# Linear attention's rows multiplied by their gates in an earlier stage of a hybrid encoder layer

## The chip, the cores and the metric

The kernel runs on one core of a Trainium2 chip. A core has five engines with an instruction stream each: TensorE (PE; its weight loads are listed apart as PEld), VectorE (DVE), ScalarE (ACT), GpSimd (POOL) and SyncE (SP). SP issues nearly all of the transfers (DMAs) of this kernel. An engine runs its instructions in order and waits where one of them needs what is not there yet. The metric is the device time of one execution in microseconds (us); less is better.

## The reference, cut to what matters

One inference step of an encoder layer with two groups of heads side by side: latent attention and gated linear attention. 1024 tokens of a new stream and 64 of a running one go through it together, 1088 in all. The width is 1024; each group gives 512 of the 1024 columns that the output projection reads.

```python
def gla_mixer(q, k, v, gate_lr, r, s0, ...):
    ...
    o, s_new = gla_recurrence(q, k, v, log_a, s0)
    o = rms_norm(o, g_gla_out.reshape(GLA_HEADS, GLA_DV))
    return o.reshape(B, T, GLA_WIDTH) * silu(r), s_new

def encoder_layer(x, c, ...):
    ...
    proj = h @ w_in                       # q latents, key latents, rotary key, GLA's q, k, v, gates, r
    a_out, latent_new, krope_new = mla_mixer(...)
    b_out, s_new = gla_mixer(gq, gk, gv, g_lr, g_r, ...)
    x = x + gate1 * (concatenate([a_out, b_out]) @ w_out)
    h2 = rms_norm(x, g_norm2) * (1 + scale2) + shift2
    x = x + gate2 * (square(relu(h2 @ w_up)) @ w_down)
```

The change is about `* silu(r)`: 512 rows by 1088 tokens, multiplied elementwise before `w_out`.

## The kernel before

Activations are kept transposed: features on the 128 partitions, tokens along the free axis. A float32 product is made of three matmuls of rounded parts (`mm3`, L94 to L96): `split` (L102, L103) rounds the operand on ACT to a high part and subtracts it on DVE for a low part.

Stages follow each other: the input projection, linear attention with the key latents, the query latents' stage (262 to 345 us), attention (345 to 540), the output projection with the second norm (540 to some 640), the MLP up and down (to the end). Within a stage, generators ("streams") yield a TensorE price, a time to wait and a condition; `interleave` (L47) takes the first that is ready by its own count and so writes out the order of the work. The scheduler below it moves instructions on an engine unless they are pinned by `keep_in_program_order`. The order is fixed when the kernel is built, and so is the order in which SP issues transfers.

Two tensors in DRAM carry the columns for the output projection. `mix_d` holds 8 blocks of 128 rows: blocks 0 to 3 are attention's results, not yet divided by the sums of their rows, whose reciprocals lie in `rs_d`; blocks 4 to 7 are linear attention's normalized results, without `silu(r)`. `r_d` holds `r`.

- **`gates()`** (L1371), a stream of the latents' stage: four steps of 272 tokens. A step loads `r` (four blocks, two places), takes Silu on ACT (L1379) and stores it back to `r_d` (L1380). Behind the last step ACT loads the table for exponentials. Beside it on the engines: `cn` and `lat` (the normalized key latent, L701, L705), `cl`, which goes to `lat_d` and comes back as `latr` for the keys; `kn`, `kl`, `kh`, `kr` (keys, L996 to L1025), `cq` (query latents, L1365), stored to `cq_d`. TensorE transposes `cn` (L715) and the keys (L1014).
- **`out_early()`** (L1284), a stream of the attention stage: the first 272 tokens of the output projection's operand are loaded, multiplied by their factor (`gate`, L1278: attention's rows by `rs_d`, the others by `r_d`), and split.
- **`main()`** (L1442): the output projection in four turns `w` of 272 tokens (`WORDER`, 0, 2, 1, 3). A turn has `mx` (two tiles of four blocks; four places, so two turns), `mr` (the gates, two places) and `mb` (the reciprocals for attention's rows, one place). `gate(mx[0], mb)` and `gate(mx[1], mr)` run on DVE as products of 128x1088, then `split` makes `mh` and `ml`. While turn `w` runs, the loads of `mr`, `mb` and `x` for turn `w + 1` and of `mx` for `w + 2` are issued.
- **`norm2()`**: per turn, the sum of squares `acc` becomes `st` (DVE L1526, a power on POOL L1527), `dg` (DVE L1530: a diagonal), and a matmul of `dg` (L1534) that spreads it over the partitions.

Of the kernel before, what the change touches and what calls it, by code (L numbers as in the profile page):

```python
# [10 lines left out]
F32 = mybir.dt.float32  # L11
# [3 lines left out]
ALU = mybir.AluOpType  # L15
# [4 lines left out]
P = 128  # L20
# [6 lines left out]
H = 4  # L27
# [45 lines left out]
def layer(ctx: ExitStack, tc: tile.TileContext, I, O):  # L73
# [1209 lines left out]
    def out_early():  # L1283
# [18 lines left out]
        r1, t3 = fetch(r_d, 0, 2), fetch(mix_d, 3, 1)  # L1302
        yield 0, 2500, None
        pin(gate(t1, r1))
        halves(4, 2, t1)
        t2, r2 = fetch(mix_d, 6, 2), fetch(r_d, 2, 2)
# [3 lines left out]
        pin(gate(t2, r2))  # L1310
# [60 lines left out]
    def gates():  # L1371

        yield 0, 0, has("k 8", "end C1")
        for c in range(4):
            r = qp.tile([P, 4, HT // 2], F32, name="r", bufs=2)
            ts = slice(c * HT // 2, (c + 1) * HT // 2)
            SP.dma_start(r, r_d[:, :, ts])
            yield 0, 3500, None
            ACT.activation(r, r, AF.Silu)  # L1379
            SP.dma_start(r_d[:, :, ts], r)  # L1380
            yield 0, 1000, None
        tc.keep_in_program_order(ACT.preload_act_table_set("natural_log_exp_and_others"))
# [43 lines left out]
    with ExitStack() as octx:  # L1426
# [13 lines left out]
        def main():  # L1440
            ld = {}
# [10 lines left out]
            def load_gates(w):  # L1452
                if w >= 4:
                    return
                c = WORDER[w]
                ld[c] += [xw.tile([P, 4, HW], F32, name="mr", bufs=2), xw.tile([P, 4, HW], F32, name="mb", bufs=1)]
                for _, t0, n, o in place(c)[2]:
                    SP.dma_start(ld[c][3][:, :, o:o + n], sums_row(0, H, t0, n))
                    SP.dma_start(ld[c][2][:, :, o:o + n], r_d[:, :, t0:t0 + n])
# [11 lines left out]
            for w, c in enumerate(WORDER):  # L1471
                _, _, parts = place(c)
                if w == 0:
                    mh, ml = mixh[1]
                else:
                    mx = ld.pop(c)
                    mh, ml = mix_pair() if w == 2 else [xw.tile([P, 8, HW], F32R, name=f"m{x}1", bufs=1) for x in "hl"]
                    gate(mx[0], mx[3])
                    split(mh[:, 0:4], ml[:, 0:4], mx[0], DVE)
                    gate(mx[1], mx[2])  # L1480
                    split(mh[:, 4:8], ml[:, 4:8], mx[1], DVE)
                if w == 0:
                    load_x(0)
                    load_mix(1)
                load_gates(w + 1)
                load_x(w + 1)
                load_mix(w + 2)
# [588 lines left out]
```

## Time and profile before

| | us |
|---|---|
| median of 3 runs | 1329.35 |
| lowest and highest | 1327.03, 1332.3 |
| the profiled execution | 1331.06 |
| its span | 1329.2 |
| PE busy in it | 1307.7 (98%) |
| DVE busy | 911.7 (69%) |
| ACT busy | 647.2 (49%) |
| latents' stage, 262 to 345 us: PE busy, DMA share | 81.25 of 83, 0.53 |
| out projection, 538 to 600 us: PE busy, DMA share | 59.28 of 62, 0.94 |

The span runs from the first to the last instruction of the profiled execution; its time has some 1.9 us more around it. Each row of the engines' timelines begins with the start and the duration in us; a bracket at its end tells how long the engine was idle before the instruction and which instruction or transfer ended that. A row of transfers gives their count, the KB of each and, where the trace tells it, the median us from issue to landing.

### The profile page before, as it was taken

Reading aid. Unit: us, or ns where it says so; the run is one execution under the profiler, and the core shown is the slowest. Engines: PE = TensorE matmul, PEld = TensorE weight load, DVE = VectorE, ACT = ScalarE, POOL = GpSimd, SP = SyncE. Lnnn points to the kernel's source line nnn. Section 1 sums busy time; section 2 is a strip of 40 time slices with the busy share of each in tenths; the row PEclk is TensorE's granted clock in tenths of the full one; section 3 lists DMA queues with packets and bytes.
Section 4 is the critical chain, followed back from the end, with each engine's and each line's share of the span. In section 5 each row is a group of like instructions: output and inputs, shape, how many; then the busy total and the mean of one; then the engine's idle time right before and its main releaser. Section 6 shows DMA issues by size and latency. Waiting matters only on the chain.

```text
span 1329.2 us, 25834 instructions
## 1 busy us (share of the span) xinstructions
PE 1307.7 (98%) x9925; PEld 1248.1 (94%) x9925; DVE 911.7 (69%) x2032; ACT 647.2 (49%) x1608; POOL 77.7 (6%) x136
## 2 busy tenths in 40 slices
PE   9999999999999999999999999999999999999999
PEld 8899999889777889999999999999999999999998
DVE  4898787466577767576999976566546955864554
ACT  5375554564266666443765445444444343333332
POOL 0100010121112200001000000000000000000000
PEclk9999999999999999999999999999999999999999
DMA  9420123384445202792346654344259645442441
GB/s 344 147 75 1 49 77 89 97 238 128 158 131 155 74 16 81 203 283 86 99 150 210 196 172 157 124 158 140 86 206 384 223 160 193 161 127 85 135 127 35
DMA packets 164653, 191.40 MB, mean 144 GB/s; under 512 B 15686, under 2 KB 116914, under 8 KB 164402
## 3 DMA queue, kind: packets, MB, share of 16 engines
q1 hardware_dynamic: 162002, 186.46, 44.3%
q10 hardware_dynamic: 2528, 3.29, 0.7%
q8 instruction: 78, 1.28, 0.4%
q14 instruction: 45, 0.37, 0.1%
HBM read 136.22 MB, written 53.49 MB: 143 GB/s over the span
## 4 chain that ended last, share of the span: by engine, by line
PE 73%; DVE 11%; DMA 7%; ACT 5%; issue 2%; POOL 2%; SPq 0%; ACTq 0%; DVEq 0%; POOLq 0%
PE mm L94 13%; PE mm L96 12%; PE mm L95 12%; PE g L94 5%; PE g L96 5%; PE g L95 5%; PE tp L94 3%; PE tp L96 3%; PE tp L95 3%; PE mm L1094 3%; PE g L1124 2%; PE g L886 1%; PE mm L179 1%; DMA mb<-rs_d 1%; PE tp L1134 1%
## 5 line engine op out<-in xcount | busy, mean ns | idle before, releaser
L102 ACT CAST opers<-quad 128x512 fp32r<-128x512 f32 x112 | 69.5, 621 | 183.3 <-PE mm L96 147.0
L103 DVE TENSOR_TENSOR opers<-quad,opers 128x512 fp32r<-128x512 f32 x112 | 77.3, 690 | 113.7 <-ACT opers L102 113.7
L96 PE MATMUL mm<-opers 128*128 128x272 f32 x448 | 128.7, 288 | 0.0
L94 PE MATMUL mm<-opers 128*128 128x272 f32 x448 | 128.4, 287 | 0.3 <-DVE e L2003 0.3
L95 PE MATMUL mm<-opers 128*128 128x272 f32 x448 | 128.2, 286 | 0.0
L94 PE MATMUL mm<-ah,wh 128*128 128x272 f32 x424 | 121.8, 288 | 0.0
L96 PE MATMUL mm<-ah,wl 128*128 128x272 f32 x424 | 121.8, 288 | 0.0
L95 PE MATMUL mm<-al,wh 128*128 128x272 f32 x424 | 121.7, 287 | 0.0
L94 PE MATMUL mm<-hh,wh 128*128 128x384 f32 (+2 forms) x264 | 90.7, 344 | 0.1
L95 PE MATMUL mm<-hl,wh 128*128 128x384 f32 (+2 forms) x264 | 87.4, 331 | 0.0
L96 PE MATMUL mm<-hh,wl 128*128 128x384 f32 (+2 forms) x264 | 87.0, 330 | 0.0
L94 PEld LDWEIGHTS mm<-opers 128*128 128x128 f32 x448 | 84.5, 189 | 0.5 <-issue 0.5
L96 PEld LDWEIGHTS mm<-opers 128*128 128x128 f32 x448 | 84.2, 188 | 0.0
L95 PEld LDWEIGHTS mm<-opers 128*128 128x128 f32 x448 | 84.1, 188 | 0.0
L94 PEld LDWEIGHTS mm<-ah,wh 128*128 128x128 f32 x424 | 79.9, 188 | 0.0
L95 PEld LDWEIGHTS mm<-al,wh 128*128 128x128 f32 x424 | 79.7, 188 | 0.0
L103 DVE TENSOR_TENSOR opers<-ru,opers 128x544 fp32r<-128x544 f32 x108 | 77.7, 720 | 2.9 <-ACT opers L102 2.7
L96 PEld LDWEIGHTS mm<-ah,wl 128*128 128x128 f32 x424 | 79.6, 188 | 0.1
L102 ACT CAST opers<-ru 128x544 fp32r<-128x544 f32 x108 | 69.6, 645 | 14.0 <-PE mm L96 10.9
L102 ACT CAST wh<-ru 128x512 fp32r<-128x512 f32 x67 | 41.2, 620 | 66.4 <-PE tp L95 21.0
L94 PE MATMUL mm<-wh,hh 128*128 128x264 f32 (+3 forms) x216 | 65.7, 304 | 0.9 <-ACT cl L718 0.9
L96 PE MATMUL g<-opers 128*128 128x272 f32 x224 | 64.7, 289 | 0.0
(415 smaller groups left out, 4228.5 us busy)
## 6 DMA issues: line engine op xcount, KB each, us to landing
ru<-u_d SPq DMA_DIRECT2D x108, 272.0 KB, 2.8
raw<-in_w_ada SPq DMA_DIRECT2D x32, 512.0 KB, 5.3
ru<-in_w_up SPq DMA_DIRECT2D x32, 512.0 KB, 4.2
quad<-in_w_down SPq DMA_DIRECT2D x16, 1024.0 KB, 5.4
u_d<-st SPq DMA_DIRECT2D x60, 272.0 KB, 2.1
u_d<-sc SPq DMA_DIRECT2D x45, 272.0 KB, 2.2
raw<-in_w_in SPq DMA_DIRECT2D x22, 256.0 KB, 6.1
x<-in_xo_T SPq DMA_DIRECT2D x8, 544.0 KB, 7.9
```

Of the source, the lines that this page charges most:

```text
L94: pin(PE.matmul(out, lhsT=ah, rhs=bh, start=first, stop=False, skip_group_check=more))
L95: pin(PE.matmul(out, lhsT=ah, rhs=bl, start=False, stop=False, skip_group_check=more))
L96: pin(PE.matmul(out, lhsT=al, rhs=bh, start=False, stop=last, skip_group_check=more))
L102: ACT.copy(hi, src)
L103: eng.tensor_tensor(out=lo, in0=src, in1=f32(hi), op=ALU.subtract)
L179: mm = PE.matmul(acc[32 * j:32 * j + 32, 0:256], lhsT=scT[:, k, :], rhs=was[k][:, 256 * j:256 * (j + 1)], start=(k == 0), stop=(k == KT - ...
L886: PE.matmul(sc[:n, a, p], lhsT=d[:, w * p + n * a:w * p + n * a + n], rhs=qv[:, :, p, a], start=True, stop=True)
L1094: PE.matmul(sp[:n, :w], lhsT=x[:, hd, :n], rhs=y[:, hd, :w], start=(j == 0), stop=(j == 4))
L1124: PE.matmul(op[:, :n], lhsT=kvs[kt // 4].v[:kw, kt % 4, hd], rhs=pt[:kw, k, :n], start=(kt == 0), stop=(kt == nkt - 1))
L1134: PE.transpose(tp[:kw, k, :n], pr[k0 // 4][:n, P * k:P * k + kw], ident[:n, :n])
```

## The change

- `gates()` takes eight steps of 136 tokens instead of four of 272. A step loads `r` (two places, as before) and `rm`, linear attention's rows out of `mix_d` (one place), takes Silu of `r` on ACT, multiplies `rm` by it on DVE (L1381) and stores the product back to `mix_d` (L1382). Nothing is stored to `r_d` any more.
- `out_early()` loads no gates, and its two products with them are gone.
- `main()` loads no `mr`; the three products with it are gone. `mb` has three places instead of one. It is loaded two turns ahead, before the `mx` of that turn: the second turn's at the start, ahead of `load_mix(1)`.

```diff
     def gates():
 
         yield 0, 0, has("k 8", "end C1")
-        for c in range(4):
-            r = qp.tile([P, 4, HT // 2], F32, name="r", bufs=2)
-            ts = slice(c * HT // 2, (c + 1) * HT // 2)
+        for c in range(8):
+            r = qp.tile([P, 4, HT // 4], F32, name="r", bufs=2)
+            ts = slice(c * HT // 4, (c + 1) * HT // 4)
+            m = qp.tile([P, 4, HT // 4], F32, name="rm", bufs=1)
             SP.dma_start(r, r_d[:, :, ts])
-            yield 0, 3500, None
+            SP.dma_start(m, mix_d[:, 4:8, ts])
+            yield 0, 2500, None
             ACT.activation(r, r, AF.Silu)
-            SP.dma_start(r_d[:, :, ts], r)
+            yield 0, 1000, None
+            DVE.tensor_tensor(out=m, in0=m, in1=r, op=ALU.mult)
+            SP.dma_start(mix_d[:, 4:8, ts], m)
             yield 0, 1000, None
...
         b0, t0, t1 = fetch(rs_d, 0, 3), fetch(mix_d, 0, 3), fetch(mix_d, 4, 2)
         fetch(rs_d, 3, 1, b3)
         yield 0, 5000, None
         pin(gate(t0, b0))
         halves(0, 3, t0)
-        r1, t3 = fetch(r_d, 0, 2), fetch(mix_d, 3, 1)
+        t3 = fetch(mix_d, 3, 1)
         yield 0, 2500, None
-        pin(gate(t1, r1))
         halves(4, 2, t1)
-        t2, r2 = fetch(mix_d, 6, 2), fetch(r_d, 2, 2)
+        t2 = fetch(mix_d, 6, 2)
         pin(gate(t3, b3))
         halves(3, 1, t3)
         yield 0, 3000, None
-        pin(gate(t2, r2))
         halves(6, 2, t2)
...
-            def load_gates(w):
+            def load_sums(w):
                 if w >= 4:
                     return
                 c = WORDER[w]
-                ld[c] += [xw.tile([P, 4, HW], F32, name="mr", bufs=2), xw.tile([P, 4, HW], F32, name="mb", bufs=1)]
+                rows[c] = xw.tile([P, 4, HW], F32, name="mb", bufs=3)
                 for _, t0, n, o in place(c)[2]:
-                    SP.dma_start(ld[c][3][:, :, o:o + n], sums_row(0, H, t0, n))
-                    SP.dma_start(ld[c][2][:, :, o:o + n], r_d[:, :, t0:t0 + n])
+                    SP.dma_start(rows[c][:, :, o:o + n], sums_row(0, H, t0, n))
...
-                    gate(mx[0], mx[3])
+                    gate(mx[0], rows.pop(c))
                     split(mh[:, 0:4], ml[:, 0:4], mx[0], DVE)
-                    gate(mx[1], mx[2])
                     split(mh[:, 4:8], ml[:, 4:8], mx[1], DVE)
                 if w == 0:
                     load_x(0)
+                    load_sums(1)
                     load_mix(1)
-                load_gates(w + 1)
                 load_x(w + 1)
+                load_sums(w + 2)
                 load_mix(w + 2)
```

SP in the latents' stage, where the third and the fourth step of the gates run (`kraw` is the rotary key, `latr` the key latents coming back). Before, with the loads and the stores of both steps in pairs:

```order
L1377 DMA r<-r_d 128x4x272 x2
L709 DMA out_kr_p<-kraw 128x64
L719 DMA lat_d<-cl 256x1x128
L955 DMA latr<-lat_d 128x2x128
L1380 DMA r_d<-r 512x1x272 x2
L719 DMA lat_d<-cl 256x1x128
L709 DMA out_kr_p<-kraw 128x64
```

Now, from the third step's load of `rm` to the fourth step's store (`r` is loaded a step ahead):

```order
L1376 DMA r<-r_d 128x4x136
L1377 DMA rm<-mix_d 128x4x136
L1382 DMA mix_d<-rm 128x4x136
L719 DMA lat_d<-cl 256x1x128
L709 DMA out_kr_p<-kraw 128x64
L1376 DMA r<-r_d 128x4x136
L1377 DMA rm<-mix_d 128x4x136
L955 DMA latr<-lat_d 128x2x128
L1382 DMA mix_d<-rm 128x4x136
```

Each store of `rm` now stands ahead of the next load of `rm`, and the transfers of the keys stand between them in the same queue.

DVE in the same stage, between the keys (`kn`, `krt`) and two key latents (`cn`, `lat`). Before:

```order
L1007 TENSOR_TENSOR kn<-kn,ssk 128x256
L1008 TENSOR_TENSOR krt<-kraw,ssk 128x256
L701 TENSOR_SCALAR cn<-mm,s_3438 128x256
L705 TENSOR_TENSOR lat<-cn,gkv_bc 128x256
L1365 TENSOR_SCALAR cq<-mm,vT 128x320
L701 TENSOR_SCALAR cn<-mm,s_3499 128x256
L705 TENSOR_TENSOR lat<-cn,gkv_bc 128x256
```

Now:

```order
L1007 TENSOR_TENSOR kn<-kn,ssk 128x256
L1008 TENSOR_TENSOR krt<-kraw,ssk 128x256
L1381 TENSOR_TENSOR rm<-rm,r 128x544
L701 TENSOR_SCALAR cn<-mm,s_3438 128x256
L705 TENSOR_TENSOR lat<-cn,gkv_bc 128x256
L1363 TENSOR_SCALAR cq<-mm,vT 128x320
L1381 TENSOR_TENSOR rm<-rm,r 128x544
L701 TENSOR_SCALAR cn<-mm,s_3499 128x256
L705 TENSOR_TENSOR lat<-cn,gkv_bc 128x256
```

The fourth and the fifth product with the gates stand three instructions apart here, each ahead of a `cn`.

DVE in the output projection, at the first norm (`st`, `dg`), in the second turn's time; the numbers tell the tiles apart. Before:

```order
L1509 TENSOR_TENSOR acc_6814<-acc_6814,sq_6872 128x272
L1278 TENSOR_TENSOR mx_6649<-mx_6649,mb_6805 128x1088
L1501 SCALAR_TENSOR_TENSOR x21_6607<-mm_6875,modT_98,x21_6607 128x208
L1501 SCALAR_TENSOR_TENSOR x21_6607<-mm_6875,modT_98,x21_6607 128x64
L1526 TENSOR_SCALAR st_6914<-tp_6910 128x2
L1526 TENSOR_SCALAR st_6914<-tp_6910 16x1
L1278 TENSOR_TENSOR mx_6650<-mx_6650,mr_6804 128x1088
L1509 TENSOR_TENSOR acc_6814<-acc_6814,sq_6903 128x272
L1530 TENSOR_SCALAR dg_6919<-ident_73,st_6914 128x128 x2
```

Now:

```order
L1510 TENSOR_TENSOR acc_6844<-acc_6844,sq_6902 128x272
L1278 TENSOR_TENSOR mx_6840<-mx_6840,mb_6838 128x1088
L1502 SCALAR_TENSOR_TENSOR x21_6641<-mm_6905,modT_98,x21_6641 128x208
L1502 SCALAR_TENSOR_TENSOR x21_6641<-mm_6905,modT_98,x21_6641 128x64
L1527 TENSOR_SCALAR st_6944<-tp_6940 128x2
L1527 TENSOR_SCALAR st_6944<-tp_6940 16x1
L1531 TENSOR_SCALAR dg_6949<-ident_73,st_6944 128x128 x2
```

`mx_6649` is the third turn's operand, `mx_6840` the fourth's. The third turn's product with `mb` now stands one turn earlier, ahead of the last two `x` of the first turn, and no product stands between `st` and `dg`.

More of the change, by code (lines that the diff above doesn't have):

```diff
@@ L1440, in main @@
         def main():
-            ld = {}
+            ld, rows = {}, {}
             def load_mix(w):
```

## The prediction

> **What bounds the kernel now.** I read the page first, then TensorE's waits, then the two stages that the change touches.
>
> ```profile
> span 1329.2 us, 25834 instructions
> PE 1307.7 (98%) x9925; PEld 1248.1 (94%) x9925; DVE 911.7 (69%) x2032; ACT 647.2 (49%) x1608; POOL 77.7 (6%) x136
> ...
> PE tp L1534 <- DVE dg L1530: 1.4, 1, 1.4
> PE mm L95 <- DVE ml L103: 1.2, 1, 1.2
> PE mm L94 <- ACT cl L718: 0.9, 1, 0.9
> ```
>
> TensorE is busy 98% of the span, so work taken off VectorE, ScalarE or the queues is worth only the TensorE waits that it ends, and work put on them costs only the waits that it makes. The three waits shown (engine and line that waited, what it waited for, total, times, longest) stand where the change acts: the first two in the out projection's stage, the third in the latents' stage. All that can be won there is some 3.5 us plus what the clock adds:
>
> ```profile
> 262.00:345.00 83.00, 81.25 (x508) 76.21 (x510) 48.93 (x121) 41.52 (x131) 17.28 (x35) 1.00 0.53 158
> 538.00:600.00 62.00, 59.28 (x457) 58.22 (x456) 41.13 (x79) 24.67 (x45) 2.63 (x2) 0.97 0.94 258
> 567.00:570.41 3.41, 2.24 (x18) 2.03 (x17) 3.41 (x5) 1.52 (x3) 0.00 (x0) 1.00 1.13 355
> 581.78:585.19 3.41, 2.02 (x14) 1.65 (x14) 2.75 (x8) 1.84 (x4) 2.44 (x2) 1.00 1.12 364
> 585.19:588.60 3.41, 3.41 (x16) 3.41 (x16) 3.41 (x8) 1.94 (x5) 0.00 (x0) 0.50 1.09 275
> ```
>
> The columns are the stretch, its length, PE, PEld, DVE, ACT and POOL busy, the granted clock, the DMA share and GB/s. The latents' stage (first row) idles TensorE for 1.75 of 83 us and leaves the DMA engines half free; in the out stage they are 94% busy. After 3.41 us in which TensorE worked 2.02, the clock was 0.50 for the next 3.41, which costs half of that, 1.7 us; after 3.41 us with 2.24 of work it stayed at 1.00.
>
> **The latents' stage: eight multiplies through one place.** In the change `rm` has one place, so each turn runs in a ring: VectorE's multiply, the store of `rm`, the next load into the same place, the next multiply. SP issues store and load in its order, and VectorE keeps its own. The prices:
>
> ```profile
> L103 DVE TENSOR_TENSOR opers<-ru,opers 128x544 fp32r<-128x544 f32 x108 | 77.7, 720 | 2.9 <-ACT opers L102 2.7
> ru<-u_d SPq DMA_DIRECT2D x108, 272.0 KB, 2.8
> r_d<-r SPq DMA_DIRECT2D x4, 544.0 KB, 4.8
> lat_d<-cl SPq DMA_DIRECT2D x8, 128.0 KB, 2.1
> L1377 SPq DMA_DIRECT2D r<-r_d x4: 557/574/773, 265.2 to 284.7; - x4
> ```
>
> A multiply of 128x544 takes 0.72. The store of 272 KB lies between 2.1 (128 KB) and 4.8 (544 KB, the stage's own gates); by size that is 3.0; I take 2.6, between it and the 2.1, which most stores of the stage are near. The load takes 2.8 (same size), each issue 0.57. A turn is 0.72 + 2.6 + 0.57 + 2.8 + 0.57 = 7.2 us; with 2.1 and one issue hidden 6.2, with 4.8 both ways 11.
>
> The Trainium skill ("DMA: Bandwidth & Descriptors", Anatomy of one DMA) gives a transfer about 2.0 us fixed and the rest by its bytes, and under Rules for kernel authors says to coalesce many small ones. It would estimate 2.6 for each leg and a turn of 7.1; its rule speaks against halving the steps, and the 2.1 for 128 KB against 4.8 for 544 KB agrees that the fixed part is large.
>
> Is there room? The rows after which VectorE's order now has multiplies 3 to 8:
>
> ```profile
> 290.93 0.75 DVE L1016 SCALAR_TENSOR_TENSOR kl<-tp,vT,kh 128x512 fp32r<-128x512 f32 x1 [3.54 <-ACT kh L1015]
> 299.61 0.42 DVE L1008 TENSOR_TENSOR krt<-kraw,ssk 128x256 f32<-128x256 f32 x1
> 301.34 0.54 DVE L1365 TENSOR_SCALAR cq<-mm,vT 128x320 f32<-128x320 f32 x1
> 304.20 0.48 DVE L701 TENSOR_SCALAR cn<-mm,s 128x256 f32<-128x256 f32 x1 [2.32 <-POOL s L122]
> 311.57 0.76 DVE L996 COPY kn<-g 128x256 f32<-128x256 f32 x2
> 318.04 0.75 DVE L1016 SCALAR_TENSOR_TENSOR kl<-tp,vT,kh 128x512 fp32r<-128x512 f32 x1
> 325.40 0.41 DVE L996 COPY kn<-g 64x256 f32<-64x256 f32 x1
> 304.75 0.43 PE L715 MATMUL mm<-ident,cn 128*128 128x128 f32 x2
> 298.87 0.41 PE L94 MATMUL mm<-wh,hh 128*128 128x320 f32 x1 [0.85 <-ACT cl L718]
> 329.93 0.33 PE L1014 MATMUL tp<-ident,kn 64*128 64x64 f32 x2 [0.23 <-DVE kn L1007]
> 288.10 2.22 ACT L1379 ACTIVATE r<-r 128x1088 f32<-128x1088 f32 x2 [1.81 <-DVE lat L705]
> ```
>
> By their ends the multiplies would start at 291.7, 300.0, 301.9, 311.9, 318.8 and 325.8 (the sixth between the two copies of 311.57): apart by 8.3, 1.9, 10.0, 6.9 and 7.0. Only the fifth is far too near to the fourth. It starts 7.2 after it, at 307.2, and `cn`, behind it in VectorE's order, at 307.9 instead of 304.20. TensorE transposes that `cn` at 304.75, 0.07 after it ended, so it has no slack: +3.7. Against this stand the 0.85 before 298.87, which I let go whole, since two Silus of together 2.22 stand shortly ahead of the chain to `cl` now and only halves do then: **+2.9** (with a turn of 6.2 +1.9, of 8.3 +4.0). What waits on SP behind the ring (`lat_d`, `out_kr_p`, the latents' loads) is needed later than this. The sixth multiply stands within a `kn` chain (0.72 of work, half of it in idle time): **+0.4**. The eighth stands between the copies of the sample keys, where TensorE already waited 0.23: its 0.72, 0.2 for the room of 7.0, and its load's place behind a `cq_d` store on SP come to **+1.3** (0.7 to 2.5). And an idle stretch of some 3 us within 3.41 halved the clock at 1.39 already: **+1.7** (0 to 3.4).
>
> The Trainium skill ("TensorE: Matmul & The Clock Gate", HAM oscillation) has a rule of no idle gaps over about 3.4 us. By it a 3 us stall would cost only itself, and the sum below would be 1.7 less. The window of 2.02 busy speaks against it.
>
> **The attention's tail.** `out_early` loses two gate multiplies of 128x544 (0.72 each, as above) and two loads; the split of their rows moves ahead of the last softmax rows, and two matmuls stand earlier than their cast. The 0.16 wait below can go; in exchange TensorE can wait for that cast or those rows, for up to a subtract of 0.72 with a cast of 0.65: **+0.5** (-0.2 to +1.4).
>
> ```profile
> 546.71 0.40 PE L94 MATMUL mm<-mh,wh 128*128 128x272 f32 x1 [0.16 <-ACT mh L102]
> ```
>
> **The out projection.** Three gate multiplies of 1.28 and three `mr` loads of 544 KB go, `mb` is loaded two turns ahead.
>
> ```profile
> 566.37 1.29 DVE L1278 TENSOR_TENSOR mx<-mx,mr 128x1088 f32<-128x1088 f32 x1
> 570.74 0.50 DVE L1501 SCALAR_TENSOR_TENSOR x<-mm,modT,x 128x272 f32<-128x272 f32 x1
> 579.61 1.29 DVE L1278 TENSOR_TENSOR mx<-mx,mb 128x1088 f32<-128x1088 f32 x1 [2.39 <-DMA mb<-rs_d]
> 581.35 0.20 DVE L1526 TENSOR_SCALAR st<-tp 128x2 f32<-128x2 f32 x2
> 583.70 0.77 DVE L1530 TENSOR_SCALAR dg<-ident,st 128x128 f32<-128x128 f32 x3 [0.60 <-POOL st L1527]
> 573.08 0.41 SPq L1458 DMA_DIRECT2D mb<-rs_d  x1
> 573.55 0.56 SPq L1459 DMA_DIRECT2D mr<-r_d  x1
> 576.35 3.51 SPq L1450 DMA_DIRECT2D mx<-mix_d  x2
> DMA to landing us min/median/max: 7.3/8.7/10.1
> ```
>
> The 1.17 that TensorE waited for `ml` goes: the gate stands three rows earlier and the second one of 1.29 is gone. But the norm's `st` stands behind a gate, and this is now the gate of the fourth turn instead of the third. It waits no longer for `mb` but for its own `mx` rows. These are issued behind the first turn's stores and two loads. Without the issues of `mb` and `mr` between (0.41 + 0.56, with gaps 1.1 from 573.08 to 574.15) that is at 575.3 by the rows of before; what lands earlier without `mr` lets the stores go earlier, against which the third turn's gate now stands ahead of the last two of their evictions (570.74) and waits for its own `mx`. I take 573, land them by the median of 8.7 (last row, all loads of `mx`) at 581.7, and so the gate 2.1 later than 579.61. The chain from there (gate, `x`, `st`, GpSimd's power, `dg`) is as long as before, 579.61 to 583.70, so the matmul of `dg` comes **2.1** later than now, the 1.17 included; what is late next is only the norm itself. With 570 and 7.3 it comes back to the matmuls before it: the 1.2 and the 1.4 are won and the halved stretch too, -4.3; with 576 and 10.1 it is +6.5. The halved stretch behind it stays, with TensorE waiting over 1.4.
>
> **The sum.** 2.9 + 0.4 + 1.3 + 1.7 + 0.5 + 2.1 = +8.9. The profiled execution took 1331.06, its span 1329.2 with 1.9 around it; it stands 1.7 above the median of 1329.35, so 1340.0 beside that execution and **1338** as a median. VectorE's other work (5.8 added in the latents, 5.3 taken out later) hides under its 69%.
>
> **The rivals.**
>
> 1. The clock does not halve in the latents' stage (the stall falls on two windows; 2.24 of 3.41 was enough to keep it): all else the same, 1.7 less, 1336.5. It is the case in which the Trainium skill's rule named above ("TensorE: Matmul & The Clock Gate") holds.
>
> 2. The out projection wins although the latents lose: the fourth turn's `mx` lands by 578, as fewer loads stand in the queue (its 94% share falls by 1.6 MB of `mr`). Then -4.3 for +2.1: 1332. Against it: the queue, not the bytes, sets the issue, and the last `mx` was the slowest of all with 10.1.
>
> 3. Other side, not slower: the ring is short enough. One mechanism: store and load overlap the spacing, which the half-busy DMA engines allow, with a turn at or under 6.2 us and the stores of 2.1; then `cn` comes 2.7 late, 1.9 reach TensorE after the 0.85, the clock stays, the sample keys cost 0.7 and the out stage gives -4.3 as in 2: 1.9 + 0.4 + 0.7 - 4.3 = -1.3, 1328. It decides at a turn of about 6; it needs the fourth turn's `mx` early as well.
>
> 4. A long ring: 512 pieces in a transfer, as in the gates' old store, price each leg near 4.8 and the turn at 10 to 11. Then multiplies 4, 5, 7 and 8 all wait, `cn` by some 6.5 and the sample keys by 4: some 16 in all, 1346.
>
> **How the numbers follow.** Chances: forecast 0.42, rival 1 0.16, rival 2 0.19, rival 3 0.14, rival 4 0.09. The forecast's own range is 1334 to 1343, from a turn of 6.8 to 8.3 and the gate 0 to 4 later. The whole range goes from rival 3's 1328 up to 1343. About 0.5% (6.6 us) is what a measurement of this kernel can tell from no change: faster is under 1322.7, slower over 1336.0. Faster needs rival 3 with every cover holding: 0.04. Slower is four fifths of the forecast, just over half of rival 1 and all of rival 4, 0.52. The same is the rest, 0.44.
>
> **What would show it.** In the changed kernel's latents' stage VectorE should stand idle 2 to 6 us before the fifth `rm` multiply, released by the load of `rm`, and TensorE at the transposes of `cn` behind it 2 to 4 us; the window behind that should be at 0.50. At the norm, `dg` should end a TensorE wait of 3 to 5 us, and the gate ahead of `st` should be released by `mx`. The wait for `ml` should be gone. The forecast is wrong if a turn from multiply to multiply is shorter than 6.2, or if `mx` of the fourth turn lands before TensorE needs `dg`.

## The result, and the profile after

The changed kernel took **1342.47 us** (median of 4 runs, 1341.61 to 1342.8), the kernel before 1330.57 (4 runs, 1327.03 to 1332.3). The ratio is 1.0090 with an interval of 1.0075 to 1.0106: slower by 0.9%, some 11.9 us. The prediction said 1338, between 1328 and 1343, with slower by over 0.5% as the likeliest outcome. The profiled execution of the change lies 0.9 under its median and that of before 0.5 above its own, so the traces below show 10.3 us of the 11.9.

The page's head and the longest of TensorE's waits in the changed kernel (engine and line that waited, what it waited for, total us, times, longest):

```profile
span 1339.5 us, 25856 instructions
PE 1310.6 (98%) x9925; PEld 1251.0 (93%) x9925; DVE 912.2 (68%) x2035; ACT 646.0 (48%) x1612; POOL 75.4 (6%) x136
...
PE tp L1014 <- DVE kn L1007: 5.6, 5, 2.0
PE tp L1535 <- DVE dg L1531: 4.6, 1, 4.6
PE mm L715 <- DVE cn L701: 2.1, 1, 2.1
...
PE mm L94 <- ACT cl L718: 1.0, 1, 1.0
...
PE mm L94 <- ACT mh L102: 0.8, 1, 0.8
```

The wait for `ml` (1.2 before) is gone, as foreseen. New is the wait for `cn`; the wait for `dg` grew from 1.4 to 4.6, that for `mh` from 0.16 to 0.8, and the one for the keys `kn` more than doubled: it was 2.3 in the same view before.

**Where the time went, stage by stage.** TensorE does the same matmuls in nearly the same order in both kernels, so the start of the same matmul in the two timelines tells how far the change is behind at that point. Four such places, at the latents' start, behind the latents, early in the output projection and behind its second norm. Before:

```profile
268.02 0.32 PE L96 MATMUL mm<-wh,hl 128*128 128x320 f32 x1
350.75 0.33 PE L1014 MATMUL tp<-ident,kn 128*128 128x128 f32 x1 [0.95 <-DVE kn L1007]
548.20 0.29 PE L94 MATMUL mm<-mh,wh 128*128 128x272 f32 x1
606.89 0.59 PE L1534 MATMUL tp<-dg,ones 128*128 128x128 f32 x3
```

After:

```profile
266.68 0.32 PE L96 MATMUL mm<-wh,hl 128*128 128x320 f32 x1
357.33 0.33 PE L1014 MATMUL tp<-ident,kn 128*128 128x128 f32 x1 [0.95 <-DVE kn L1007]
555.85 0.29 PE L94 MATMUL mm<-mh,wh 128*128 128x272 f32 x1
617.21 0.59 PE L1535 MATMUL tp<-dg,ones 128*128 128x128 f32 x3
```

The first comes 1.34 earlier, then the lag is 6.58, 7.65 and 10.32, and 10.3 at the end (1339.5 against 1329.2). The 1.34 lie ahead of any changed code; in every other trace of this study, too, that place comes 0.2 to 1.3 earlier than in the one trace of before. So the latents' stage lost **7.9**, the attention with its tail **1.1**, the output projection **2.7**, and what follows nothing.

The stages and the stretches of 3.41 us in which the clock fell, in the changed kernel (stretch, length, PE, PEld, DVE, ACT and POOL busy, granted clock, DMA share, GB/s; the grid of 3.41 is counted back from the rows at 0.50):

```profile
262.00:345.00 83.00, 75.69 (x447) 70.79 (x446) 50.80 (x119) 39.90 (x129) 17.46 (x34) 0.96 0.64 181
302.06:305.48 3.42, 1.70 (x12) 1.34 (x10) 0.77 (x2) 2.26 (x6) 0.74 (x2) 1.00 0.52 139
305.48:308.89 3.41, 3.00 (x19) 2.97 (x20) 3.38 (x7) 2.39 (x7) 0.00 (x0) 1.00 0.67 174
329.37:332.79 3.42, 1.43 (x9) 1.08 (x8) 2.05 (x5) 1.38 (x10) 0.98 (x2) 1.00 0.47 155
332.79:336.20 3.41, 1.81 (x9) 1.52 (x8) 2.60 (x7) 1.03 (x3) 0.99 (x2) 0.50 0.28 83
336.20:339.62 3.42, 3.42 (x14) 3.42 (x14) 0.54 (x2) 0.26 (x1) 0.00 (x0) 0.50 0.15 58
```

TensorE's idle time in the latents' window rose from 1.75 to 7.31 (83.00 less 75.69), and two stretches ran at half clock where before there was none. They do not lie behind `cn`: the stretch with that wait (302.06) worked 1.70 of 3.42, and the next stayed at 1.00. They lie behind the sample keys, the 64-row `kn` at 330 us.

**The ring at `cn`.** Rows of SP, ACT, DVE and TensorE in the changed kernel, from the fourth multiply to the transposes of `cn`:

```profile
297.23 0.72 DVE L1381 TENSOR_TENSOR rm<-rm,r 128x544 f32<-128x544 f32 x1
297.98 0.36 SPq L1382 DMA_DIRECT2D mix_d<-rm  x1
301.77 0.38 SPq L1377 DMA_DIRECT2D rm<-mix_d  x1
302.93 0.66 ACT L1379 ACTIVATE r<-r 128x544 f32<-128x544 f32 x1 [3.52 <-DMA r<-r_d]
303.49 0.36 ACT L699 ACTIVATE cn<-mm 128x256 f32<-128x256 f32 x1
304.31 0.55 POOL L122 TENSOR_TENSOR s<-s,mhalf 128x1 f32<-128x1 f32 x1
304.71 0.73 DVE L1381 TENSOR_TENSOR rm<-rm,r 128x544 f32<-128x544 f32 x1 [4.64 <-DMA rm<-mix_d]
305.36 0.48 DVE L701 TENSOR_SCALAR cn<-mm,s 128x256 f32<-128x256 f32 x1
305.89 0.44 PE L715 MATMUL mm<-ident,cn 128*128 128x128 f32 x2 [2.13 <-DVE cn L701]
```

The fourth multiply starts at 297.23; its store is issued at 297.98, the next load of `rm` can be issued only at 301.77, when the one place is free, and the fifth multiply starts at 304.71: a turn of 7.48. `cn` stands behind it on VectorE, and TensorE waits 2.13. But there are two chains to `cn`, not one. On ACT the Silu at 302.93 waited 3.52 for its `r`, and behind it in ACT's order stands the sum of squares of that `cn` (303.49), from which GpSimd makes `s`, ready at 304.86. With that Silu where it is, `cn` could not have started before about 304.9 even without the ring, which held it to 305.36.

**The ring at the sample keys.** The seventh and the eighth multiply, in the same timelines:

```profile
322.39 0.72 DVE L1381 TENSOR_TENSOR rm<-rm,r 128x544 f32<-128x544 f32 x1 [1.99 <-DMA rm<-mix_d]
326.14 0.32 SPq L1364 DMA_DIRECT2D cq_d<-cq  x1
327.73 0.37 SPq L1377 DMA_DIRECT2D rm<-mix_d  x1
328.18 0.62 DVE L1363 TENSOR_SCALAR cq<-mm,vT 128x384 f32<-128x384 f32 x1 [1.61 <-DMA cq_d<-cq]
328.72 0.41 DVE L996 COPY kn<-g 64x256 f32<-64x256 f32 x1
330.69 0.72 DVE L1381 TENSOR_TENSOR rm<-rm,r 128x544 f32<-128x544 f32 x1 [1.57 <-DMA rm<-mix_d]
332.56 0.30 PE L1014 MATMUL tp<-ident,kn 64*128 64x64 f32 x2 [1.99 <-DVE kn L1007]
334.46 0.47 PE L1014 MATMUL tp<-ident,kn 64*128 64x64 f32 x2 [1.60 <-DVE kn L1007]
```

Here the load of `rm` also stands behind a `cq_d` store on SP (326.14), which can go only when its `cq` is made; the turn is 8.30, the multiply stands between the copies of the keys, and TensorE waits 1.99 and 1.60 where it waited 0.23 in all.

But the multiply is the smaller part of it. The first copy of these keys (328.72) stands behind a `cq`, which has one place as well and waits for its own store to `cq_d`. Before, that `cq` stood here:

```profile
324.87 0.62 DVE L1365 TENSOR_SCALAR cq<-mm,vT 128x384 f32<-128x384 f32 x1 [1.29 <-DMA cq_d<-cq]
```

The copy behind it started at 325.40, so it comes 3.3 later now, where the lag since `cn` is 1.14 (305.89 against 304.75): 2.2 are lost ahead of the multiply. The `cq` before this one had to wait for a store issued at 319.45 and started at 325.56, 6.1 later; before it was 317.77 and 322.06, 4.3. On SP a load of `rm` (318.22) stands just ahead of that store now; whether this made it land late is not shown. From the copy to the second pair of transposes the way grew by 1.2, from 4.53 (329.93 less 325.40) to 5.74, and that is the multiply with its wait.

The transfers of the ring:

```profile
rm<-mix_d SPq DMA_DIRECT2D x8, 272.0 KB, 3.6
mix_d<-rm SPq DMA_DIRECT2D x8, 272.0 KB, 3.8
```

The latents' balance: `cn` 2.13, sample keys 1.99 + 1.60 - 0.23 = 3.36 (2.2 by `cq`, 1.2 by the multiply), `cl` 0.2 more than before, and of the 6.83 us at half clock those in which TensorE worked cost half: (6.83 - 1.60) / 2 = 2.6. That is 8.3 against 7.9 measured.

**The output projection.** SP, DVE and TensorE around the first norm, and the stretches at it (columns as above):

```profile
581.16 2.01 SPq L1452 DMA_DIRECT2D mx<-mix_d  x2
590.35 1.29 DVE L1278 TENSOR_TENSOR mx<-mx,mb 128x1088 f32<-128x1088 f32 x1 [5.71 <-DMA mx<-mix_d]
593.06 0.48 DVE L1531 TENSOR_SCALAR dg<-ident,st 128x128 f32<-128x128 f32 x2 [0.76 <-POOL st L1528]
593.40 1.01 PE L1535 MATMUL tp<-dg,ones 128*128 128x128 f32 x3 [4.57 <-DVE dg L1531]
```

```profile
588.79:592.20 3.41, 0.04 (x1) 0.00 (x0) 1.85 (x5) 0.00 (x0) 0.00 (x0) 1.00 0.70 229
592.20:595.61 3.41, 2.21 (x8) 1.95 (x9) 2.01 (x9) 0.86 (x2) 1.24 (x2) 0.50 0.17 58
```

The fourth turn's `mx` is issued behind stores of `x`, at 581.16, and lands some 9.2 later, when the gate starts. The fourth turn's gate waits 5.71 for it on VectorE, and `st`, which stands behind the gate, needs nothing of it. So `dg` is late and TensorE waits 4.57; then the clock is at 0.50 from 592.20 to 599.03, two stretches, where before it was one. The balance: 4.57 - 1.4 = 3.2, less the 1.2 of `ml`, and 6.83 at half clock with 1.2 of it spent waiting, 2.8, against 1.7 before: 3.1, measured 2.7.

### The profile page after: what moved, and what is told of

Same layout as the page of the kernel before. It is cut to its first block, busy times and chain, and to the rows that moved or that the text cites. A ratio compares the mean times of both kernels' runs of the same rounds, so it can differ in the third digit from the quotient of the medians.

```text
span 1339.5 us, 25856 instructions
## 1 busy us (share of the span) xinstructions
PE 1310.6 (98%) x9925; PEld 1251.0 (93%) x9925; DVE 912.2 (68%) x2035; ACT 646.0 (48%) x1612; POOL 75.4 (6%) x136
## 3 DMA queue, kind: packets, MB, share of 16 engines
q8 instruction: 78, 1.28, 0.4%
## 4 chain that ended last, share of the span: by engine, by line
PE 73%; DVE 11%; DMA 7%; ACT 4%; issue 2%; POOL 1%; SPq 1%; ACTq 0%; DVEq 0%; POOLq 0%
PE mm L94 13%; PE mm L96 13%; PE mm L95 13%; PE g L94 5%; PE g L96 5%; PE g L95 5%; PE tp L94 3%; PE tp L96 3%; PE tp L95 3%; PE mm L1094 2%; PE g L1124 2%; PE g L886 2%; DMA mx<-mix_d 1%; PE mm L179 1%; DVE wl L106 1%
```

## The experiments

Each experiment was timed against runs of the kernel before on the same chip. The stage columns are the lag against the one trace of before, by the same four matmuls as above, in us; they are from one execution of each kernel.

| run | median us | before there | ratio (interval) | latents | attention | out proj. |
|---|---|---|---|---|---|---|
| the change | 1342.47 | 1330.57 | 1.0090 (1.0075-1.0106) | +7.9 | +1.1 | +2.7 |
| rm2 | 1337.7 | 1326.66 | 1.0087 (1.0070-1.0103) | +5.8 | +0.5 | +2.1 |
| mb1 | 1334.15 | 1326.66 | 1.0052 (1.0037-1.0067) | +7.0 | +1.2 | -4.1 |
| rm2_mb1 | 1334.68 | 1326.66 | 1.0054 (1.0033-1.0075) | +8.4 | +1.0 | -4.5 |
| out_only | 1332.55 | 1326.66 | 1.0041 (1.0026-1.0056) | +0.1 | +0.5 | +3.4 |
| r3rm2_mb1 | 1333.24 | 1328.49 | 1.0037 (1.0023-1.0050) | +7.6 | +0.5 | -4.2 |
| spaced_8 | 1335.49 | 1328.49 | 1.0046 (1.0031-1.0060) | +9.3 | +0.2 | -3.7 |
| spaced_12 | 1330.87 | 1328.49 | 1.0013 (1.0003-1.0023) | +4.6 | +0.7 | -4.2 |
| mb_behind_mx | 1335.5 | 1328.49 | 1.0047 (1.0032-1.0063) | +7.0 | +1.8 | -4.6 |
| in_attention | 1328.27 | 1328.4 | 0.9999 (0.9991-1.0008) | +0.6 | +1.2 | -4.5 |
| in_attention_mx | 1327.32 | 1328.4 | 0.9988 (0.9978-0.9997) | +2.7 | +1.7 | -4.6 |

The trace of before took 1331.06, which is more than the medians of before on the other chips (1326.66 to 1328.49). The differences of the medians are mostly larger than the stage columns add up to, by 0.2 us (the change) to 3.4 us (mb1); only for in_attention_mx are they 0.9 smaller. The gain of some 4 us in the last column stands against a single execution of before, and in times it may be worth up to 3 us less. The granted clock tells part of the reason. The traced execution of before has the stretch at half clock in its output projection, worth 1.7, and a mean clock of 0.999; of the 41 executions of before that were timed beside the experiments 30 show 1.000. One such stretch lowers the mean over 1329 us by 0.0013, so by this estimate those 30 had none. Most executions of the kernel before, then, do not lose the 1.7 that the last column counts as won.

### rm2: two places for `rm`

The theory: the ring through one place is the latents' loss. The rival: something else behind the eight steps is.

```diff
-            m = qp.tile([P, 4, HT // 4], F32, name="rm", bufs=1)
+            m = qp.tile([P, 4, HT // 4], F32, name="rm", bufs=2)
```

> The changed kernel with two places for rm instead of one, all else the same. Theory (ring of store and load through one place): the load of a step no longer waits for the store of the step before, so the idle 4.64 us ahead of the fifth multiply and the 1.6 to 2.0 ahead of the seventh and eighth go, and with them TensorE's waits for cn (2.1) and for the sample keys' kn (2.0 and 1.6, of which 0.7 stay for the eighth multiply itself) and the two halved stretches of the clock behind them (6.8 us at 0.50, worth 3.4). Sum about -7.5: 1335, with the 4.6 us wait for dg in the output projection still there. Rival (it is the eight multiplies' and transfers' own weight on VectorE and SP, not the ring): at most 2 us come back, 1340 to 1342.

Measured: ratio 1.0087, as slow as the change. No multiply waits for `rm` any more, and the latents still lost 5.8. Rows of its timelines, and the stretches there:

```profile
294.40 1.35 DVE L1381 TENSOR_TENSOR rm<-rm,r 128x544 f32<-128x544 f32 x2
296.19 1.24 SPq L1376 DMA_DIRECT2D r<-r_d  x2
299.61 0.66 ACT L1379 ACTIVATE r<-r 128x544 f32<-128x544 f32 x1 [2.03 <-DMA r<-r_d]
301.20 0.64 PE L94 MATMUL mm<-wh,hh 128*128 128x320 f32 x1 [4.37 <-ACT cl L718]
```

```profile
295.55:298.97 3.42, 1.28 (x8) 0.96 (x6) 2.15 (x6) 1.34 (x9) 1.73 (x4) 1.00 0.93 258
298.97:302.38 3.41, 1.18 (x4) 1.18 (x5) 1.76 (x5) 2.36 (x8) 1.24 (x3) 0.50 0.99 282
```

With a second place the steps come in pairs, two multiplies back to back. Both stores and both next loads of `r` (issued from 296.19) then go together, behind those multiplies on SP, at a DMA share of 0.93 to 0.99. The Silu waits 2.03 for `r` on ACT, `cl` stands behind that Silu, and TensorE waits 4.37 for `cl` and falls to half clock for two stretches. That is the whole loss: 4.37 less the 0.85 of before is 3.5, and the 6.83 at half clock less the 2.23 spent waiting in them, halved, are 2.3. The theory that the one place costs the latents their time fell: taking away the waits for `rm` moved the loss to `r`. The order changed with the place, though, so the run does not tell what the change itself would lose without its waits for `rm`.

### mb1: one place for `mb`, loaded one turn ahead and behind `mx`

The theory: the gate of the fourth turn, ahead of `st` in VectorE's order, holds up the norm.

```diff
-                rows[c] = xw.tile([P, 4, HW], F32, name="mb", bufs=3)
+                rows[c] = xw.tile([P, 4, HW], F32, name="mb", bufs=1)
...
-                    load_sums(1)
                     load_mix(1)
+                load_sums(w + 1)
                 load_x(w + 1)
-                load_sums(w + 2)
                 load_mix(w + 2)
```

> The changed kernel with mb in one place again, loaded one turn ahead and behind the mx of its turn, as before the change; the gates' rows stay out of the output projection. Theory (the norm's st stands behind the fourth turn's gate, which waits for its mx; that order and the queue place come from the early mb): st and dg stand ahead of that gate again, TensorE's wait for dg falls from 4.6 to under 1.5, one or both halved stretches at 592 us go: 1342.5 - 3 - 1.7 = about 1338, latents' stage unchanged. Rival (the wait comes from transfers that are slow however they are ordered): wait for dg over 3 us, 1341 to 1343.

Measured: ratio 1.0052. The wait for `dg` is gone, and so are the stretches at half clock behind it; the latents lost 7.0 as in the change. VectorE at the first norm:

```profile
588.14 0.48 DVE L1530 TENSOR_SCALAR dg<-ident,st 128x128 f32<-128x128 f32 x2 [0.76 <-POOL st L1527]
...
592.50 1.29 DVE L1278 TENSOR_TENSOR mx<-mx,mb 128x1088 f32<-128x1088 f32 x1 [3.39 <-DMA mb<-rs_d]
```

The fourth gate stands behind `dg` now. It still waits, 3.39 for `mb`, and nobody waits for it. So the output projection without the gates' rows does win, against the trace of before 4.1, as soon as the fourth turn's product does not stand ahead of `st`.

### rm2_mb1: both

```diff
-            m = qp.tile([P, 4, HT // 4], F32, name="rm", bufs=1)
+            m = qp.tile([P, 4, HT // 4], F32, name="rm", bufs=2)
...
-                rows[c] = xw.tile([P, 4, HW], F32, name="mb", bufs=3)
+                rows[c] = xw.tile([P, 4, HW], F32, name="mb", bufs=1)
```

(with `mb1`'s order of loads)

> Both edits together. Theory: the two losses are apart, so their gains add: 1342.5 - 7.5 - 4.5 = 1330.5, within 2 us of the kernel before; since gate multiplies and mr loads are out of the output projection it can come 1 to 3 us under it (1328 to 1330). Rival (the move itself costs, whatever the places): 1335 or more.

Measured: ratio 1.0054, the same as mb1 alone within the intervals, and TensorE waits 4.8 for `cl` as in rm2. A time within 2 us of the kernel before was expected, and it is 8.0 above: the second place is worth nothing with either order of the output projection.

### out_only: the latents' stage of before, the rest of the change

```diff
-        for c in range(8):
+        for c in range(4):
...
-            SP.dma_start(m, mix_d[:, 4:8, ts])
...
-            DVE.tensor_tensor(out=m, in0=m, in1=r, op=ALU.mult)
-            SP.dma_start(mix_d[:, 4:8, ts], m)
+            SP.dma_start(r_d[:, :, ts], r)
```

> The latents' stage of the kernel before (four Silu steps that write r back) with the changed output projection. Leaves out the multiplication of linear attention's rows by the gates. Theory (latents' stage lost about 7.9 us, output projection the other 2.5 to 3.5): 1330.6 + 3 = 1333.5, the wait for dg 4 to 5 us with the halved stretches behind it, no waits for cn or the sample keys. Rival (the late latents' stage alone makes the output projection late, by where SP's and VectorE's work falls): 1330 to 1331, wait for dg under 2.

The kernel leaves out the factor `silu(r)`. Measured: ratio 1.0041. The latents lost 0.1, the output projection 3.4, by the same wait:

```profile
PE tp L1531 <- DVE dg L1527: 5.1, 1, 5.1
```

So the two losses are separate: the eight steps make the latents', and the output projection loses its own without help from the lag before it.

### r3rm2_mb1: three places for `r`, two for `rm`

The theory after rm2: the Silu lacks a place for `r`.

```diff
-            r = qp.tile([P, 4, HT // 4], F32, name="r", bufs=2)
+            r = qp.tile([P, 4, HT // 4], F32, name="r", bufs=3)
...
-            m = qp.tile([P, 4, HT // 4], F32, name="rm", bufs=1)
+            m = qp.tile([P, 4, HT // 4], F32, name="rm", bufs=2)
```

(on mb1)

> The kernel mb1 with three places for r and two for rm in the latents' stage. First theory (rings through too few places, of rm and of r): with both rings widened ScalarE no longer waits for r (2 to 3.5 us at a time in the kernels so far) and VectorE not for rm; the latents' stage loses under 2 us against before instead of 7 to 8, ratio to before 0.998 to 1.000. New theory (the scheduler places Silu and multiply for a load that it takes to be shorter than it is; more places only let it pack the steps closer, so that the in-order engines wait for r instead): the stage still loses 4 to 9 us, ratio 1.003 to 1.007.

Measured: ratio 1.0037; the latents lost 7.6, and both kinds of wait are back: `r` holds up a Silu ahead of `cl` (1.56 at 300.76), `rm` a multiply (1.65 at 303.16), and TensorE waits 6.38 for `cl`:

```profile
303.78 0.64 PE L94 MATMUL mm<-wh,hh 128*128 128x320 f32 x1 [6.38 <-ACT cl L718]
```

With more places the order puts the steps closer: the last Silu starts at 300.8 here and at 301.0 in rm2, at 318.4 in the change. Here ACT's load of the table for exponentials (1.28, at 301.44), which follows the last Silu, comes ahead of that `cl` as well. So more places do not take the loss away. That left the theory that the work of a step stands too soon behind its own loads in ACT's and VectorE's orders.

### spaced_8 and spaced_12: the steps further apart in the order

Both take mb1's output projection and keep one place for `rm`. The stream of the gates is put first, starts at "end C1", has its instructions held in the written order, and waits longer between load, Silu, multiply and next load. spaced_8 (spaced_12 has 6500 behind the loads, 2500 behind the Silu and 3000 behind the store):

```diff
-        yield 0, 0, has("k 8", "end C1")
+        yield 0, 0, has("end C1")
...
-            SP.dma_start(r, r_d[:, :, ts])
-            SP.dma_start(m, mix_d[:, 4:8, ts])
+            tc.keep_in_program_order(SP.dma_start(r, r_d[:, :, ts]))
+            tc.keep_in_program_order(SP.dma_start(m, mix_d[:, 4:8, ts]))
+            yield 0, 4500, None
+            tc.keep_in_program_order(ACT.activation(r, r, AF.Silu))
+            yield 0, 1500, None
+            tc.keep_in_program_order(DVE.tensor_tensor(out=m, in0=m, in1=r, op=ALU.mult))
+            tc.keep_in_program_order(SP.dma_start(mix_d[:, 4:8, ts], m))
             yield 0, 2500, None
...
-        interleave([weights, rotations(), past_keys(), lats, query_main(), query_latents(), gates()], rest=(weights,))
+        interleave([weights, gates(), rotations(), past_keys(), lats, query_main(), query_latents()], rest=(weights,))
```

> The kernel mb1, places of r and rm as in the change (2 and 1), but the eight steps are written out first among the stage's streams, their instructions pinned to that order, one step every 8.5 us (4.5 from loads to Silu, 1.5 to the multiply, 2.5 to the next loads). New theory (each load needs more time before its Silu and multiply in the order): with 8.5 a step, just over the 7.2 to 8.3 that a turn took, some waits stay: the stage loses 3 to 6 us, ratio 1.000 to 1.003. First theory (only the places count): as mb1, 1.005.

> As the kernel with 8.5 us a step, with 12 us a step (6.5, 2.5, 3.0); otherwise the same, same places. New theory: loads and stores have landed before Silu, multiply and the next load need them; the latents' stage loses at most 1 us, no halved clock there, and the output projection keeps the 4.1 us that mb1 won: 2 to 3 us under the kernel before, ratio 0.998 (0.997 to 0.999). First theory (one place of rm makes a ring that costs 7 whatever the order): 1.004 to 1.005.

Measured: spaced_8 lost 9.3 in the latents (ratio 1.0046), more than mb1 and than expected; spaced_12 lost 4.6 (ratio 1.0013, against 1.0052 for mb1), where at most 1 was expected. In spaced_12 the multiplies wait 0.6 for `rm` in all (10.8 in the change), the Silus still 4.5 for `r` (10.0 in the change), `cn` and `cl` have left TensorE's list, and what is left are the keys. The first row is from TensorE's waits in spaced_12, the second from its VectorE timeline:

```profile
PE tp L1014 <- DVE kn L1007: 5.8, 7, 1.3
```

```profile
328.55 0.71 DVE L1381 TENSOR_TENSOR rm<-rm,r 128x544 f32<-128x544 f32 x1
```

The multiply of 0.71 at 328.55 still stands inside the chain of the sample keys, now without a wait of its own; from the first copy to the second transposes the way is 0.7 longer than before, which is its duration. The copy itself comes another 1.4 late, behind a `cq` that waited 2.73 for its place, and the clock falls once behind the keys. The stage's 4.6 are these waits and that stretch: TensorE's waits in it come to 4.56 where they were 1.65, and the stretch costs 1.7. So distance helped against the waits for `rm`, and a multiply within a chain that has no slack costs its place.

In spaced_8 the distances did not reach: the multiplies still wait 4.6 for `rm`, the Silus 5.9 for `r`. It has a multiply within two chains of keys that hold up TensorE (2.18 and 0.92 at 318.94 and 320.26, 2.21 at 336.08). The first of these chains is late for another reason too: VectorE waited 3.00 there for `kr`, which ACT makes behind a `cl` that waited 3.08 for its own store to `lat_d`.

### mb_behind_mx: the three places and two turns kept, `mx` issued first

This asks whether mb1 won by its place and lead or by the order of the loads.

```diff
-                    load_sums(1)
                     load_mix(1)
+                    load_sums(1)
                 load_x(w + 1)
-                load_sums(w + 2)
                 load_mix(w + 2)
+                load_sums(w + 2)
```

> The changed kernel with the two loads of a turn swapped: mx of a turn first, then mb; three places and the lead of two turns are kept. If the queue order of mb ahead of mx made the norm's wait (by making the fourth turn's operand late and its gate stand ahead of st): TensorE's wait for dg goes as in mb1, the output projection wins 3 to 4 us against before, ratio 1.005. If the lead or the three places made it: wait for dg 4 to 5 us, ratio 1.009 as the change.

Measured: ratio 1.0047, the output projection 4.6 less than before. The fourth gate again stands behind `dg`, whose own row starts at 587.58:

```profile
590.17 1.29 DVE L1278 TENSOR_TENSOR mx<-mx,mb 128x1088 f32<-128x1088 f32 x1 [1.62 <-DMA mb<-rs_d]
```

So it is neither the places nor the lead: the same loads with their issue exchanged give the same as mb1. That the order takes the fourth gate for earlier than it can be when `mb` is issued ahead of `mx` is the reading that fits; what the scheduler reckoned with was not looked at.

### in_attention and in_attention_mx: the products moved out of the latents

The latents' stage is that of before (four steps, Silu stored to `r_d`). The eight products, one place each for `gr` and `gm`, run in the attention stage, where VectorE's order has room, and `out_early` waits for the last. The output projection is mb1's in the first, mb_behind_mx's in the second.

```diff
+    def gate_rows():
+
+        yield 0, 0, None
+        for c in range(8):
+            r = qw.tile([P, 4, HT // 4], F32, name="gr", bufs=1)
+            m = qw.tile([P, 4, HT // 4], F32, name="gm", bufs=1)
...
+            yield 0, 6000, None
             DVE.tensor_tensor(out=m, in0=m, in1=r, op=ALU.mult)
             SP.dma_start(mix_d[:, 4:8, ts], m)
+            yield 0, 9000, None
+        done.add("gated")
```

> The latents' stage of the kernel before (four Silu steps that write r back to DRAM); linear attention's rows are multiplied by the gates in eight steps of 136 tokens during the attention stage instead (loads of r and of the rows, multiply on VectorE, store), one place each; output projection without gates and with mb in one place, as in mb1. Theory (the move costs only where the in-order engines wait for its transfers; in the attention stage their order leaves time): latents' stage 0, attention +0.5 to +1.5, output projection -4.1 to -4.6: 3 us under the kernel before, ratio 0.9965 to 0.9985. Rival (a gate multiply through DRAM costs some 7 us wherever it is put): 1.002 to 1.005.

> The same with the output projection of the kernel mb_behind_mx (three places for mb, two turns ahead, issued behind the mx of its turn). Theory: as its sister with mb in one place, output projection -4.6 instead of -4.1; ratio 0.996 to 0.998. Rival (the early mb costs): 0.999 or more.

Measured: ratios 0.9999 and 0.9988, both above what was expected. By the traces in_attention is what its theory said: the latents lost 0.6, the attention 1.2, and the output projection won 4.5; the ratio lacks, in part, the 1.7 that most executions of before do not lose. The same multiply, through one place, waits for nothing in in_attention, although its load takes 4.5 there and its store 4.8, longer than in the latents. `dg` and `cn` are not among TensorE's waits, and the keys have 1.5 of them (2.3 before).

In in_attention_mx the latents lost 2.7 and the attention 1.7. No product with the gates runs in those latents, yet the copy of the sample keys comes 1.0 late behind a `cq` that waited 1.67 for its place, TensorE waits 1.22, and a stretch ran at half clock behind it. So this place can cost as much by itself. It need not: the traced execution is the slowest of this kernel's eleven (1329.76) and has a mean clock of 0.999, and nine of them show 1.000.

in_attention_mx is the only kernel of the study whose interval lies below 1: some 1.0% below the change by the two ratios, and 0.12% below before, just clear of it, and not clear of its sister. With that the change's idea pays for itself at best and hardly more.

## Why the prediction was right or wrong

**The side was right, and so were the places of the lag:** `cn` and the sample keys in the latents, and the fourth turn's gate ahead of `st` in the output projection. The runs mb1 and out_only part the two stages cleanly. The mechanism was right in the output projection; in the latents the ring of `rm` was only a part of it. Point by point:

- *A turn of 7.2.* Measured 7.48 from the fourth to the fifth multiply and 8.30 from the seventh to the eighth. The legs differ: from the store's issue at 297.98 to the next load's 3.8 (expected 3.2), from there to the multiply 2.9 (expected 3.4).
- *`cn` +2.9.* TensorE waited 2.13, and the wait for `cl` of 0.85, which was let go whole, stayed at 1.0: +2.3 together. The size is near. The reason was half the truth: the step that said only VectorE's order holds up `cn` left out ACT. The Silu's wait for `r` would have held it to about 304.9 by itself, 0.5 less than the ring did, and rm2 points the same way: no wait for `rm`, and 5.8 lost all the same, by a Silu that waits for `r`. The prediction worked out when each multiply can start from the ring of `rm` alone, and never asked when `r` can be there.
- *The sample keys +1.3.* **Mis-sized:** 3.4. The multiply with its wait made 1.2 of them, about what the term said, with a turn of 8.30 instead of 7.2. The other 2.2 are a wait that the prediction did not have: `cq` waits for its own store, and the keys' first copy stands behind it on VectorE. The prediction took the `cq_d` store only for what the load of `rm` stands behind on SP. In spaced_12 the two parts are 0.7 and 1.4.
- *The sixth multiply in a `kn` chain +0.4.* No wait of TensorE stands there in the change.
- *The clock +1.7 behind `cn`.* **Wrong place, and too small:** the stretch of 1.70 busy was followed by 1.00, and the clock fell behind the sample keys instead, for two stretches, 2.6.
- *The attention's tail +0.5.* The wait for `mh` grew by 0.7, as in the mechanism named; the whole stage with its tail lost 1.1, within the bound of 1.4.
- *The output projection +2.1.* Measured 2.7. The issue of the fourth turn's `mx` at 573 by the rows of before was 581.16 less the lag of 7.65, 573.5; landing 9.2 where 8.7 was taken; `dg` came 1.7 later than before (593.06 - 7.65 against 583.70) where 2.1 was forecast. The chain from gate to `dg` was not as long as before but shorter, 2.71 instead of 4.09: the two are equal up to `st` (1.75 and 1.74), and from `st` to `dg` it is 0.96 instead of 2.35, where a gate and an `acc` stood between and `dg` waited for GpSimd's power in both. The wait was 4.57, foreseen as 3 to 5. What was not counted is the second stretch at half clock.

**The sum** of 8.9 stood against 10.3 in the profiled spans and 11.9 in the medians; 1342.47 lies near the upper end of 1334 to 1343. The two terms that failed are the sample keys (2.1 too low) and the clock (in both stages together 2.0 too low); `cn` was 0.6 too high, the sixth multiply 0.4. That the total came out within the range is in part luck: the range was drawn for a longer turn and a later gate, and what filled it were `cq` and two more stretches at half clock.

**The rivals.** The first, that the clock does not fall in the latents, held at `cn` and failed at the keys. The Trainium skill ("TensorE: Matmul & The Clock Gate", HAM oscillation) sets the limit at gaps of about 3.4 us; the trace disagrees, since the longest gap in the stretch from 329.37 was 1.99 and the next ran at 0.50. The second, that the output projection wins 4.3, failed in the change, and was the right figure for what is there: mb1 and mb_behind_mx gave 4.1 and 4.6 against the trace of before. Its condition was not the one met: not that `mx` landed early, but that the gate stood behind `dg`. The third (turn at or under 6) failed with the 7.5 to 8.3. The fourth, a ring of 10 to 11, did not come.

**What stays open.** In the latents the load of `r` and the load of `rm` each hold `cn` up by about as much, and no run took away the wait for `r` alone. At the sample keys no run gave `cq` a second place, and why its store landed late is not shown: the copy is 1.8 to 2.3 late in the change, mb1 and mb_behind_mx, which all load `rm` there, but also 1.0 and 1.1 late in in_attention_mx and rm2_mb1, which do not. The eight steps in the attention were not priced: the 1.2 and 1.7 there are within the 0.2 to 1.8 of the kernels without them.

## What to carry to other kernels

Work that waits for a transfer holds up everything behind it on its in-order engine, so before moving such work into a busy stage ask for each of its engines (here the Silu's as well as the multiply's) what stands behind it and when its load can be issued at the earliest, the place that must come free included. Other rings through one place that share the queue, here `cq` and its store, belong to the question. More places are no cure where the order then packs the steps closer; a distance of 12 us in the order helped, one of 8.5 did not, and another stage took nearly all of the loss away. And when two loads feed one product, the order in which they are issued can decide where the scheduler puts the product: exchanging their issue took the output projection from +2.7 to -4.6 in the traces, and the ratio from 1.0090 to 1.0047.

## What the runs showed of the hardware that was not expected

The granted clock does not follow the busy share of the stretch before in a plain way. With 1.70 of 3.42 busy (the change at 302.06) and with 1.61 and 1.66 (spaced_8 at 315.14 and 332.21) the next stretch stayed at 1.00; with 1.43 and 0.04 (the change), 1.28 (rm2), 2.02 (before) and even 2.25 (spaced_8 at 335.63) it fell to 0.50. Once at 0.50 it stayed there for another stretch where TensorE had idled in the first (1.81, 2.21 and 1.18 busy, two stretches each), and was back at 1.00 behind a first stretch that was busy throughout (3.41 in before, 3.42 in spaced_12). So the stall of 2.13 at `cn` cost nothing more, and the two of 1.99 and 1.60 at the keys cost 2.6 more.

The same 272 KB took 3.6 to load and 3.8 to store in the latents, and 4.5 and 4.8 in the attention, where the loads of `ru` of the same size in the trace of before took 2.8. The Trainium skill ("DMA: Bandwidth & Descriptors", Anatomy of one DMA) has a fit, made for transfers that GpSimd issues, by which an estimate for each is 2.6. These are issued by SP, and the medians of `rm` and `gm` were 3.0 to 4.8 in every run but one: the stores of `rm` in spaced_8 took 2.4.
